# Attention scores: the second pass over the keys on 64 contraction rows, two heads side by side

## The chip, the cores and the metric

The kernel runs on one core of a Trainium2 chip. The metric is the device time of one execution in microseconds (us). Engines are named as in the profile: PE is TensorE's matmul stream and PEld its weight load, DVE is VectorE, ACT is ScalarE, POOL is GpSimd, and SP issues the DMAs.

## What is computed

The reference is two layers of a hybrid block over 2048 latent tokens and 256 context tokens of width 1024. Each layer normalises and modulates its input, projects it, runs three groups of heads in parallel (windowed attention, Fourier mixing, a short convolution), gates and concatenates them, and projects the result back with a residual add. The change is in the attention, whose core is this:

```python
def window_attention(q, k, v, kc, vc, sink_b):
    ...
    qb = (q * (HEAD_DIM ** -0.5)).reshape(b, nb, BLOCK, KV_HEADS, Q_PER_KV, HEAD_DIM).transpose(1, 0, 2, 3, 4, 5)
    ...
    def one_block(args):
        ...
        s_loc = jnp.einsum('bqkgd,bnkd->bkgqn', qi, ks).astype(jnp.float32)
        s_loc = jnp.where(valid, s_loc, -jnp.inf)
        s_ctx = jnp.einsum('bqkgd,bnkd->bkgqn', qi, kc).astype(jnp.float32)
        p = sink_softmax(jnp.concatenate([s_ctx, s_loc], axis=-1), sink_b).astype(v.dtype)
        return (jnp.einsum('bkgqn,bnkd->bqkgd', p[..., :nc], vc)
                + jnp.einsum('bkgqn,bnkd->bqkgd', p[..., nc:], vs))
```

There are 8 query heads of 64 dimensions, which share 2 key/value heads (four query heads each). A block is 128 query tokens. It sees all 256 context keys and its own block with the neighbour on each side: 384 local keys, or 256 at the two ends of the sequence. In the first layer the 256 context tokens are updated too, as two blocks that see the context keys alone.

## The kernel before, in words

**Precision.** Matmul operands are of type fp32r, whose products are less exact than fp32. Each operand is therefore split into hi and lo (`split`, L79: hi is the rounded copy, lo the rest), and a product is formed as hi*hi + hi*lo + lo*hi, three matmuls (`proj_k`, L274). For the attention scores the split is folded into the contraction: a head has only 64 dimensions, and the array contracts 128 rows. So q is stored in DRAM with hi in rows 0 to 63 and lo in rows 64 to 127 of every head (`store_hl`, L299; `dst` is `qs`, 128 rows x 8 heads x tokens). The keys are loaded twice, once into rows 0 to 63 and once into rows 64 to 127 (`open_ep` L1033 for the context keys, `kseg` L1211 for the local ones), each copy with hi and lo as separate planes, index `x`.

**Scores.** `u_qk` (L1067) makes the scores of one block and one key/value head, four query heads `hh` in turn. For each it takes a PSUM tile `sp` of two banks and runs two passes over the context keys (L1078, 256 columns) and two over the local keys (L1081, 384 or 256 columns). With x = 0 all 128 rows contract [q hi; q lo] with key hi in both halves, with x = 1 the same rows contract with key lo. Then DVE reads the tile once, adds the mask and finds the row maximum (L1088), and ACT takes the exponential (L1091). After the fourth head POOL scales by the reciprocal of the sums (L1102).

**Order.** Layer by layer there are two phases: `half` (projections, Fourier mixing, convolution) and `phase2` (attention and output projection). In `phase2` every stage runs several generators whose calls are interleaved by a string; one letter is one call:

```python
ORDER = "bAACCBCcBCABBACBBCBBCcACBCBB"
```

A is `u_qk` of the current unit (block and key/value head), B is `u_pv` of the unit before (transposes of the probabilities L1127, their split on ACT and DVE, the product with the values L1140 and L1141), C is `u_out` (output projection L1176 to L1178, norm, residual); small letters are the same generators of the stage before, being finished. So PE gets its instructions in an order written out by hand, and it runs them in that order. The A calls stand at places 2, 3, 11, 14 and 23: the first four are the four heads, the last takes the reciprocal and has POOL scale. The first stages and the last have strings of their own of the same kind.

**PSUM.** There are two `sp` tiles; each is free again when DVE has read it (L1088). `tp` has two banks, `op` and `yp` one each, and that fills PSUM.

Of the kernel before, what the change touches and what calls it, by code (L numbers as in the profile page):

```python
# [8 lines left out]
F32 = mybir.dt.float32  # L9
# [54 lines left out]
def f(t):  # L64
    return t.bitcast(F32)


class Kern:
# [230 lines left out]
    def store_hl(self, hi, lo, dst, tok, n, kq):  # L299
        nc = self.nc  # L300
        if kq is None:
            for v in range(2):
                for x, t in enumerate((hi, lo)):
                    nc.sync.dma_start(dst[:, v, x, tok:tok + n], f(t[v * 64:(v + 1) * 64, :n]))
        else:
            for v in range(2):
                for x, t in enumerate((hi, lo)):
                    nc.sync.dma_start(dst[x * 64:(x + 1) * 64, kq + 4 * v, tok:tok + n], f(t[v * 64:(v + 1) * 64, :n]))

    def qk_chunk(self, l, st, a, n, tok, kq, rope):  # L310
        nc = self.nc
# [755 lines left out]
    def u_qk(self, p, ps, B, kv):  # L1067
        nc = self.nc
        nm = p.tile([128, 4], F32, name="nm", tag="nm", bufs=2)
        sm = p.tile([128, 4], F32, name="sm", tag="sm", bufs=2)  # L1070
        B.pts = getattr(B, "pts", {})
        B.pts[kv] = []
        W, nl = B.W, B.nl
        for hh in range(4):
            h = kv * 4 + hh
            sp = ps.tile([128, 1024], F32, name="sp", tag="sp")
            for x in range(2):
                nc.tensor.matmul(sp[:, 256:512], B.q[:, h, :], self.kctx[:, kv, x, :], start=(x == 0), stop=(x == 1))  # L1078
            if nl:
                for x in range(2):  # L1080
                    nc.tensor.matmul(sp[:, 512:512 + nl], B.q[:, h, :], B.seg[:, kv, x, B.k0:B.k0 + nl],  # L1081
                                     start=(x == 0), stop=(x == 1))
            pt = p.tile([128, 640], F32, name="pt", tag="pt", bufs=8)[:, :W]
            d, x, m = pt, sp[:, 256:256 + W], self.mask[:, :W]
            if nl and B.qb == 0:
                d, x = [t.rearrange("p (a b) -> p a b", a=2) for t in (d, x)]
                m = self.mask.rearrange("p (a b) -> p a b", a=2)[:, :, :256]
            nc.vector.tensor_tensor_reduce(d, x, m, scale=-0.125,  # L1088
                                           scalar=self.nsink[:, h:h + 1], op0=ALU.add, op1=ALU.min,
                                           accum_out=nm[:, hh:hh + 1])  # L1090
            nc.scalar.activation(pt, pt, AF.Exp, bias=nm[:, hh:hh + 1], scale=-1.0, accum_out=sm[:, hh:hh + 1])  # L1091
            B.pts[kv].append(pt)
            if hh == 3:
                es = p.tile([128, 4], F32, name="es", tag="es", bufs=2)
                nc.gpsimd.tensor_tensor(es, nm, self.nsink[:, kv * 4:kv * 4 + 4], op=ALU.subtract)
                nc.scalar.activation(es, es, AF.Exp, bias=0.0, scale=1.0)
                nc.gpsimd.tensor_tensor(es, es, sm, op=ALU.add)
                yield
                rv = p.tile([128, 4], F32, name="rv", tag="rv", bufs=2)
                nc.vector.reciprocal(rv, es)  # L1100
                for g in range(4):
                    nc.gpsimd.tensor_scalar(B.pts[kv][g], B.pts[kv][g], rv[:, g:g + 1], 1.0, op0=ALU.mult, op1=ALU.mult)  # L1102
            yield
# [389 lines left out]
```

## Time and profile before

| | |
|---|---|
| time, median of 3 runs | 2089.26 us (2084.22 to 2091.58) |
| profiled execution, span | 2093.9 us |
| PE busy | 1980.6 us, 95% |
| DVE busy | 1233.3 us, 59% |
| second phase, first layer (676 to 1200 us) | PE 509.63 of 524 us |
| second phase, second layer (1646 to 2094 us) | PE 429.75 of 448 us |
| score matmuls, context keys (L1078) | 544 |
| score matmuls, local keys (L1081) | 512 |

The span is the time from the first to the last instruction of one execution under the profiler; the page gives no other time of that execution. Busy time of PE is taken from recorded matmuls whose ends are modelled and overlap the next matmul, so what a matmul takes in a dense stretch is read from the distance between two starts.

### The profile page before, as it was taken

The page shows a single profiled execution, that of the slowest core. Times are in us where ns is not written, and L with a number is a line of the kernel's source. Part 1 is how long each engine was busy: PE and PEld are TensorE (multiplying, and loading weights), DVE is VectorE, ACT ScalarE, POOL GpSimd, SP SyncE. Part 2 cuts the span into 40 slices and gives each one's busy share as a digit, 9 for nine tenths or more (in the row PEclk, how much of TensorE's full clock was granted, in tenths as well). Part 3 has the DMA queues.
Part 4 walks back from the last instruction along what each step waited for, and adds up shares of the span by engine and source line. Part 5 has one row for each costly group of instructions (what it writes and reads, how often), then busy time and mean ns, then how long its engine had stood idle before and what let it go on. Part 6 is the DMA issues. An engine that isn't in the chain of part 4 may idle for free.

```text
span 2093.9 us, 28506 instructions
## 1 busy us (share of the span) xinstructions
PE 1980.6 (95%) x10218; PEld 1671.9 (80%) x10218; DVE 1233.3 (59%) x2218; ACT 855.5 (41%) x1745; POOL 748.0 (36%) x967
## 2 busy tenths in 40 slices
PE   6787999999999899999999999999999989999998
PEld 2686877788788688888887888888887778888886
DVE  7343876445552677777777614333554277777775
ACT  6241211321322556666666412132222266666663
POOL 4221322231432444444444414233243254444443
PEclk9899999999999999999999999999999999999999
DMA  7678666444735744433332625124564654434421
GB/s 303 114 192 223 188 211 219 140 154 137 210 127 163 207 116 122 120 106 106 103 104 106 206 80 130 61 95 122 157 186 136 178 157 113 106 107 111 117 75 41
DMA packets 190333, 295.68 MB, mean 141 GB/s; under 512 B 17624, under 2 KB 121840, under 8 KB 189168
## 3 DMA queue, kind: packets, MB, share of 16 engines
q1 hardware_dynamic: 190192, 293.87, 47.8%
q8 instruction: 80, 1.31, 0.3%
q14 instruction: 61, 0.50, 0.1%
HBM read 218.43 MB, written 75.39 MB: 140 GB/s over the span
## 4 chain that ended last, share of the span: by engine, by line
PE 69%; DMA 10%; DVE 10%; issue 4%; POOL 3%; ACT 2%; SPq 1%; POOLq 0%; DVEq 0%; ACTq 0%
PE acc L280 8%; PE acc L279 8%; PE acc L278 8%; PE tp L1127 6%; PE yp L1176 6%; PE yp L1178 6%; PE yp L1177 6%; PE sp L1081 4%; PE op L1141 3%; PE op L1140 3%; PE sp L1078 3%; PE accb L378 2%; PE accb L376 2%; PE accb L377 2%; DVE jm L161 2%
## 5 line engine op out<-in xcount | busy, mean ns | idle before, releaser
L278 PE MATMUL acc<-big,wh 128*128 128x512 f32 x1152 | 458.9, 399 | 30.6 <-ACT big L267 11.5
L280 PE MATMUL acc<-big,wl 128*128 128x512 f32 x1152 | 454.6, 395 | 4.2 <-POOL wl L90 2.9
L279 PE MATMUL acc<-big,wh 128*128 128x512 f32 x1152 | 455.0, 395 | 0.4 <-POOL big L90 0.4
L90 POOL TENSOR_TENSOR wl<-wr,wh 128x1024 fp32r<-128x1024 f32 x63 | 158.4, 2515 | 400.5 <-ACT wh L84 272.7
L88 DVE TENSOR_TENSOR pl<-tp,ph 128x512 fp32r<-128x512 f32 x320 | 219.2, 687 | 105.6 <-ACT ph L84 102.5
L278 PEld LDWEIGHTS acc<-big,wh 128*128 128x128 f32 x1152 | 219.7, 191 | 75.2 <-ACT big L267 12.0
L1091 ACT ACTIVATE pt<-pt,nm 128x640 f32<-128x640 f32 (+2 forms) x272 | 216.2, 795 | 118.6 <-DVE nm L1088 118.2
L280 PEld LDWEIGHTS acc<-big,wl 128*128 128x128 f32 x1152 | 219.3, 190 | 51.8 <-POOL wl L90 4.0
L279 PEld LDWEIGHTS acc<-big,wh 128*128 128x128 f32 x1152 | 219.7, 191 | 43.7 <-POOL big L90 1.0
L84 ACT ACTIVATE ph<-tp 128x512 fp32r<-128x512 f32 x320 | 188.4, 591 | 132.6 <-PE tp L1127 126.2
L1102 POOL TENSOR_SCALAR pt<-pt,rv 128x640 f32<-128x640 f32 (+2 forms) x272 | 214.2, 808 | 27.2 <-DVE rv L1100 24.2
L1088 DVE CUSTOM_DVE_ANT_0 pt<-sp,mask,nsink 128x640 f32<-128x640 f32 (+2 forms) x256 | 213.4, 841 | 10.1 <-PE sp L1078 5.2
L1127 PE MATMUL tp<-ident,pt 128*128 128x128 f32 x1280 | 196.8, 274 | 12.7 <-POOL pt L1102 12.2
L1127 PEld LDWEIGHTS tp<-ident,pt 128*128 128x128 f32 x1280 | 158.6, 140 | 59.9 <-POOL pt L1102 19.2
L323 POOL TENSOR_TENSOR rs<-rs,sinT 128x512 f32<-128x512 f32 x40 | 68.1, 1703 | 183.6 <-DVE rs L321 154.1
L1081 PE MATMUL sp<-kseg,qt 128*128 128x384 f32 (+1 forms) x512 | 127.5, 330 | 1.1 <-DMA kseg<-ks 1.1
L1176 PE MATMUL yp<-big,hfh 128*128 128x512 f32 x272 | 118.1, 434 | 1.5 <-ACT big L84 1.5
L1078 PE MATMUL sp<-kctx,qt 128*128 128x256 f32 x544 | 114.2, 291 | 3.9 <-DMA qt<-qs 2.1
L1176 PE MATMUL yp<-big,hah 128*128 128x512 f32 x272 | 117.0, 431 | 0.0
L1078 PEld LDWEIGHTS sp<-kctx,qt 128*128 128x128 f32 x544 | 95.3, 189 | 18.4 <-DVE nm L1088 3.3
L1178 PE MATMUL yp<-big,hfl 128*128 128x512 f32 x272 | 107.5, 395 | 0.2
L1177 PE MATMUL yp<-big,hfh 128*128 128x512 f32 x272 | 107.1, 394 | 0.0
(373 smaller groups left out, 3711.5 us busy)
## 6 DMA issues: line engine op xcount, KB each, us to landing
wr<-in_wina SPq DMA_DIRECT2D x76, 512.0 KB, 3.8
qt<-qs SPq DMA_DIRECT2D x34, 512.0 KB, 5.0
wmt<-in_wmodt SPq DMA_DIRECT2D x32, 512.0 KB, 4.2
ftb<-ftd SPq DMA_DIRECT2D x36, 384.0 KB, 3.8
xt<-in_x SPq DMA_DIRECT2D x26, 512.0 KB, 6.4
kseg<-ks SPq DMA_DIRECT2D x24, 512.0 KB, 8.7
xt<-x SPq DMA_DIRECT2D x24, 512.0 KB, 4.5
gat<-gas SPq DMA_DIRECT2D x34, 256.0 KB, 3.2
```

The source lines that it names most:

```text
L88: self.last_v = nc.vector.tensor_tensor(lo, src, f(hi), op=ALU.subtract)
L278: nc.tensor.matmul(a, wh[:, k, :], hi[:, k, :n], start=(k == 0), stop=False)
L279: nc.tensor.matmul(a, wh[:, k, :], lo[:, k, :n], start=False, stop=False)
L280: nc.tensor.matmul(a, wl[:, k, :], hi[:, k, :n], start=False, stop=(k == KT - 1))
L1078: nc.tensor.matmul(sp[:, 256:512], B.q[:, h, :], self.kctx[:, kv, x, :], start=(x == 0), stop=(x == 1))
L1088: nc.vector.tensor_tensor_reduce(d, x, m, scale=-0.125, scalar=self.nsink[:, h:h + 1], op0=ALU.add, op1=ALU.min, accum_out=nm[:, hh:hh + 1])
L1091: nc.scalar.activation(pt, pt, AF.Exp, bias=nm[:, hh:hh + 1], scale=-1.0, accum_out=sm[:, hh:hh + 1])
L1102: nc.gpsimd.tensor_scalar(B.pts[kv][g], B.pts[kv][g], rv[:, g:g + 1], 1.0, op0=ALU.mult, op1=ALU.mult)
L1127: nc.tensor.transpose(tp[:, hh * 128:(hh + 1) * 128], pts[hh][:, t * 128:(t + 1) * 128], self.ident)
L1176: nc.tensor.matmul(yp, hh, wh[:, k, :], start=(i == 0), stop=False)
L1177: nc.tensor.matmul(yp, hh, wl[:, k, :], start=False, stop=False)
L1178: nc.tensor.matmul(yp, hl, wh[:, k, :], start=False, stop=(i == KT - 1))
```

## The change

The heads are taken in pairs, an even and an odd one. At the even head both `sp` tiles are taken, and PE gets the work of both heads: first the first pass of each over all 128 rows, then the second pass. The second pass contracts only q hi with key lo, on 64 rows; the product of q lo with key lo is no longer formed. So that the two heads lie in different halves of the array, `store_hl` writes hi of an odd head into rows 64 to 127 and lo into rows 0 to 63. For the first pass this makes no difference, since both halves of the keys hold the same. In the second pass the even head reads rows 0 to 63 and the odd head rows 64 to 127, and the matmuls of the two alternate: context keys of the even head, of the odd head, then local keys of each. At the odd head no matmul is left; the DVE and ACT work stays in its place.

```diff
@@ store_hl
-                    nc.sync.dma_start(dst[x * 64:(x + 1) * 64, kq + 4 * v, tok:tok + n], f(t[v * 64:(v + 1) * 64, :n]))
+                    r = (x + kq) % 2 * 64
+                    nc.sync.dma_start(dst[r:r + 64, kq + 4 * v, tok:tok + n], f(t[v * 64:(v + 1) * 64, :n]))
@@ u_qk
+        sps = {}
         for hh in range(4):
             h = kv * 4 + hh
-            sp = ps.tile([128, 1024], F32, name="sp", tag="sp")
-            for x in range(2):
-                nc.tensor.matmul(sp[:, 256:512], B.q[:, h, :], self.kctx[:, kv, x, :], start=(x == 0), stop=(x == 1))
-            if nl:
-                for x in range(2):
-                    nc.tensor.matmul(sp[:, 512:512 + nl], B.q[:, h, :], B.seg[:, kv, x, B.k0:B.k0 + nl],
-                                     start=(x == 0), stop=(x == 1))
+            if hh % 2 == 0:
+                for g in (hh, hh + 1):
+                    sp = sps[g] = ps.tile([128, 1024], F32, name="sp", tag="sp")
+                    q = B.q[:, kv * 4 + g, :]
+                    nc.tensor.matmul(sp[:, 256:512], q, self.kctx[:, kv, 0, :], start=True, stop=False)
+                    if nl:
+                        nc.tensor.matmul(sp[:, 512:512 + nl], q, B.seg[:, kv, 0, B.k0:B.k0 + nl], start=True, stop=False)
+                for g in (hh, hh + 1):
+                    r = slice(g % 2 * 64, g % 2 * 64 + 64)
+                    nc.tensor.matmul(sps[g][:, 256:512], B.q[r, kv * 4 + g, :], self.kctx[r, kv, 1, :],
+                                     start=False, stop=True)
+                if nl:
+                    for g in (hh, hh + 1):
+                        r = slice(g % 2 * 64, g % 2 * 64 + 64)
+                        nc.tensor.matmul(sps[g][:, 512:512 + nl], B.q[r, kv * 4 + g, :], B.seg[r, kv, 1, B.k0:B.k0 + nl],
+                                         start=False, stop=True)
+            sp = sps[hh]
```

## The prediction

> **What bounds the kernel now.** I read the summary first: which engine is full.
>
> ```profile
> span 2093.9 us, 28506 instructions
> PE 1980.6 (95%) x10218; PEld 1671.9 (80%) x10218; DVE 1233.3 (59%) x2218; ACT 855.5 (41%) x1745; POOL 748.0 (36%) x967
> ```
>
> PE, the matmul stream, is busy 95% of the span; PEld, its weight load, runs beside it. A matmul's recorded end is modelled, so only its start is used below. Next come the stretches in which the scores are computed, the second phase of each layer, from the view of busy time by stretches (core time, PE, PEld, DVE, ACT, POOL, clock, DMA share, GB/s).
>
> ```profile
> 676.00:1200.00 524.00, 509.63 (x2794) 430.73 (x2793) 386.55 (x719) 311.19 (x682) 234.24 (x424) 1.00 0.44 131
> ...
> 1646.00:2094.00 448.00, 429.75 (x2360) 363.74 (x2358) 314.78 (x590) 253.16 (x557) 184.41 (x336) 0.99 0.40 112
> ```
>
> PE has 14 us idle of 524 and 18 of 448, at full clock; the next engine, DVE, is at 70 to 74%. The chain of waits over 30 us inside names PE lines alone:
>
> ```profile
> by line: PE tp L1127 16.0%; PE yp L1176 15.6%; PE yp L1178 15.4%; PE yp L1177 15.3%; PE sp L1081 11.6%; PE op L1140 9.3%; PE op L1141 9.2%; PE sp L1078 7.9%
> ```
>
> So in these stages a nanosecond of PE's stream, gained or lost, is a nanosecond of time. The scores (L1078, L1081) are about a fifth of that stream, and half of them is the second pass.
>
> **The change part by part.** How many matmuls are touched stands in the groups, shapes kept apart:
>
> ```profile
> L1081 PE MATMUL sp<-kseg,qt 128*128 128x384 f32 x448 | 114.5, 336 | 0.0
> L1078 PE MATMUL sp<-kctx,qt 128*128 128x256 f32 x544 | 114.2, 291 | 3.9 <-DMA qt<-qs 2.1 <-DVE nm L1088 1.4 <-issue 0.4
> ...
> L1081 PE MATMUL sp<-kseg,qt 128*128 128x256 f32 x64 | 13.0, 285 | 1.1 <-DMA kseg<-ks 1.1
> ```
>
> One pair of heads has 4 context matmuls, so 544 make 136 pairs. 448/4 = 112 of these pairs have local keys of 384 columns, 64/4 = 16 of 256, and 8 (context blocks) have none. What a matmul really takes is the distance between starts in the timeline, not its recorded 291 or 336 ns:
>
> ```profile
> 901.67 0.40 PE L1078 MATMUL sp<-kctx,qt 128*128 128x256 f32 x2
> ...
> 901.91 0.51 PE L1081 MATMUL sp<-kseg,qt 128*128 128x384 f32 x2
> ...
> 902.26 0.40 PE L1078 MATMUL sp<-kctx,qt 128*128 128x256 f32 x2
> ...
> 902.50 0.51 PE L1081 MATMUL sp<-kseg,qt 128*128 128x384 f32 x2
> ...
> 902.85 0.40 PE L1176 MATMUL yp<-big,hfh 128*128 128x512 f32 x1
> ```
>
> Two of 256 columns take 0.24 us, 0.12 each; two of 384 take 0.35, 0.175 each. The second pass of a pair therefore costs 2 x 0.12 + 2 x 0.175 = 0.59 us now (0.48 with 256 local columns, 0.24 without local keys). The change keeps the number of matmuls and weight loads, but issues these four on 64 rows, heads alternating between the two halves of the array. If both halves stream at once, 0.59 becomes 0.295 (0.24, 0.12), a gain of as much.
>
> What it adds: PE goes from 128 rows to 64 and back once per pair. No 64-row matmul is in this trace. The nearest are the sixteen four-row ones of L667, in groups of four, and one group stands between full matmuls:
>
> ```profile
> 52.16 0.19 PEld L280 LDWEIGHTS acc<-big,wpl 128*128 128x128 f32 x1
> ...
> 52.40 0.40 PE L280 MATMUL acc<-big,wpl 128*128 128x512 f32 x1
> ...
> 52.73 0.32 PEld L667 LDWEIGHTS pmc<-ident,sg 4*128 4x128 f32 x4 [0.37 <-ACT jk L245]
> 52.73 0.41 PE L667 MATMUL pmc<-ident,sg 4*128 4x4 f32 x4
> 53.06 0.14 PEld L230 LDWEIGHTS pt<-ident,xt 128*128 128x128 f32 x1
> ```
> ```profile
> L667 PEld LDWEIGHTS pmc<-ident,sg x16: 133/136/138, 13.9 to 52.9; 4*128 4x128 f32 x16
> ```
> ```profile
> L662 ACT COPY sg<-pmr x2: 576/576/577, 43.1 to 50.8; 4x512 f32<-4x512 f32 x2
> ```
>
> A 512-column matmul streams 0.23 us (next fence: 237.02 to 237.25), so the L280 at 52.40 was through at 52.63. Its successor's load should start with it, at 52.40, as the load at 52.16 did with the matmul before it. It starts at 52.73: 0.10 after the stream's end. Its data can't be the reason, for the copy into sg began at 50.8 and takes 0.576. (The row blames an ACT operation that was over by 52.40; that leaves the rest unexplained.) On the way out, four loads span 0.32 with 0.136 for the last, so they start 0.06 apart and the last at 52.91; the full-row load follows at 53.06, 0.15 later in place of 0.06: another 0.09. Few columns alone don't do this; a transpose of 16 columns over all 128 rows was prefetched as any other:
>
> ```profile
> 237.02 0.39 PE L280 MATMUL acc<-big,wl 128*128 128x512 f32 x1
> 237.02 0.09 PEld L188 LDWEIGHTS pgt<-ident,gg 128*16 128x16 f32 x1
> 237.25 0.27 PE L188 MATMUL pgt<-ident,gg 128*16 128x128 f32 x1
> ```
>
> A load that isn't prefetched is paid in full. After short transposes such a one is seen:
>
> ```profile
> 904.56 0.19 PEld L1176 LDWEIGHTS yp<-big,hfh 128*128 128x128 f32 x1
> 904.59 0.48 PE L1176 MATMUL yp<-big,hfh 128*128 128x512 f32 x1
> ...
> 904.90 0.39 PE L1177 MATMUL yp<-big,hfh 128*128 128x512 f32 x1
> ```
>
> From the load to the next matmul's start are 0.34 us, of which 0.23 is the stream: the load took 0.11. So a switch costs 0.10 + 0.11 = 0.21 us, in and out 0.42 per pair. The bounds are 0 (64 rows behave as 128 do) and 0.42 (as four rows do); I take 0.42, since L667 is the one row here with part of the rows.
>
> "TensorEngine Tiling (Array Packing)" in the Trainium skill, Key Properties, speaks against this change too: changing the tiling mode, not just the tile, drains TensorE. It gives no price; by that rule the sum is the +19 us below and without it the -38 of the second rival, and the 0.10 us around L667 agrees with the rule.
>
> What the four matmuls take between the switches is bounded as well: 0.295 if both heads' loads and streams run side by side, 0.59 if nothing does. Between them is the case in which the streams overlap but four loads of 0.11 follow one another: loads end at 0.11, 0.22, 0.33, 0.44; the last local matmul starts at 0.44 and ends at 0.615, the first load included. I take 0.295 as the forecast's value, because the two halves share no rows; no row shows loads or streams of two row groups together.
>
> **The sum**: with 384 columns 0.42 - 0.295 = +0.125 us x 112 = 14.0; with 256 columns 0.42 - 0.24 = +0.18 x 16 = 2.9; context blocks 0.42 - 0.12 = +0.30 x 8 = 2.4. Together +19.3 us. Nothing hides it, as PE is the chain.
>
> What is moved: the fourth head's matmuls go ahead of two calls of the other generators, to the third's, and need the second head's PSUM buffer earlier.
>
> ```profile
> 904.62 0.88 DVE L1088 CUSTOM_DVE_ANT_0 pt<-sp,mask,nsink 128x640 f32<-128x640 f32 x1
> ...
> 906.50 0.40 PE L1078 MATMUL sp<-kctx,qt 128*128 128x256 f32 x2
> ```
>
> DVE has read that buffer by 905.50, and the pair starts at 906.50: 1 us of cover, nothing paid. If DVE slid past it, PE would stand with all the output projection's matmuls queued behind, and their ACT and DVE readers after them. Also, a first head's scores are ready only when the second's are, about 0.6 us later. DVE took the pair's first scores at 903.21, the new pair would be through near 901.67 + 1.30 = 902.97 plus the pipe: at most some tenths, hidden by the 1 us again. The stores of q swap row halves, with the same count and bytes; cost nothing.
>
> ```profile
> qs<-qh SPq DMA_DIRECT2D x64, 128.0 KB, 2.4
> ```
>
> **The rivals.**
> (a) Switch paid, little overlap. With loads in a row, a pair costs 0.10 + 0.615 + 0.10 + 0.11 - 0.59 = +0.335 x 112 = 37.5; with 256 columns the inner part is 0.56, +0.39 x 16 = 6.2; without local keys 0.34, +0.41 x 8 = 3.3: +47 us. With no overlap at all, the change not doing what it says, 0.42 x 136 = +57. For it: the 0.11 per load against 0.12 per context matmul leaves hardly room to overlap. Against: separate rows.
> (b) The other side, faster: no switch cost. Place: the same start of the pair's second pass; it decides at a switch below 0.147 us, half of 0.295. With full overlap -0.295 x 112 - 0.24 x 16 - 0.12 x 8 = -38 us, 2051. With loads in a row and one ahead, as full-row loads go now, the four take about 0.505, 0.45 and 0.23: -0.085 x 112 - 0.03 x 16 = -10 us, 2079. Against it: L667, entry and exit alike. For it: four rows may be another mode than 64. "TensorE: Matmul & The Clock Gate" (the Trainium skill), Part 3, has matmuls in distinct row groups start about 4 ns apart and names no switch cost; no run here shows it.
> (c) Neither: no switch cost and no overlap: 0 us, 2089.
>
> **How the numbers follow.** The profiled span, 2093.9, lies 4.6 over the median of 2089.26 (runs 2084.22 to 2091.58); the page shows no time around it. The sum is in absolute us of PE and I add it to the median: 2089.26 + 19.3 = 2108.6. Chances: forecast 0.32; (a) with loads in a row 0.21, without overlap 0.17; (b) full 0.13, in a row 0.09; (c) 0.08. The switch has thus 0.70, resting on one kind of row. Slower is 0.70, faster 0.22, same 0.08, where 0.3% (6 us) is about what a measurement here can tell from no change. The range leaves out full (b): from 2079 less the runs' spread of 7 us, 2072, to 2146 plus the same, 2153. The forecast alone would be 2100 to 2118.
>
> **What would show it.** In the timeline: the first 64-row load about 0.10 us after the full stream ends, not with its start; the two heads' matmuls starting within 0.06 us (overlap) or 0.11 and more (loads in a row); the next full-row load 0.10 us after the last 64-row stream. From first score matmul to the next full stream a pair takes 1.18 us now, 1.30 by the forecast, 1.51 and 1.60 by (a), 0.89 by (b). DVE waiting for the scores or PE for the buffer at over 10 us in the list of waits would say that the moved work counts. The forecast is wrong if the 64-row load starts with the full matmul ahead of it.

## The result, and the profile after

| | time, median | runs |
|---|---|---|
| kernel before | 2090.42 us | 4 (2084.22 to 2091.98) |
| kernel after | 2162.61 us | 4 (2158.92 to 2171.39) |

The ratio is 1.0361, 95% interval 1.0335 to 1.0387: 72 us slower, where 19 us were forecast and 2153 was the end of the range. The profiled execution of the kernel after took 2158.92 us, with a span of 2157.1.

Three things are read from the profile after: how busy PE is, what it waits for, and then one pair of heads at a time. First the summary of the kernel after:

```profile
span 2157.1 us, 28511 instructions
...
PE 2016.8 (93%) x10218; PEld 1638.8 (76%) x10218; DVE 1238.6 (57%) x2218; ACT 857.6 (40%) x1745; POOL 744.9 (35%) x967
```

PE's share fell from 95 to 93% though its busy time rose by 36 us (2016.8 - 1980.6). So there seem to be two losses: PE works longer, and PE stands more. The first is only a hint, because busy time rests on modelled ends: e3 below, which has no 64-row matmul, shows 2009.2 us, also 29 over before. The list of PE's waits (line waited for: us in total, times, longest) has a new first row in the kernel after:

```profile
PE sp L1082 <- DVE nm L1100: 44.9, 58, 2.5
```

The same wait in the kernel before, where the reading is L1088:

```profile
PE sp L1078 <- DVE nm L1088: 1.4, 1, 1.4
```

The first pass of a pair waits 58 times for DVE to have read the PSUM buffer. The chain of waits of the kernel after shows that this reaches the end, for POOL and DVE have grown in it from 3% and 10% in the kernel before:

```profile
PE 53%; DVE 15%; POOL 10%; DMA 9%; issue 9%; ACT 4%; SPq 2%; POOLq 0%; DVEq 0%; ACTq 0%
```

**A pair that does not wait** is the first of a unit. Timeline of PE, kernel after (start, duration, instruction, count; the start is what is read):

```profile
910.00 0.28 PE L1082 MATMUL sp<-kctx,qt 128*128 128x256 f32 x1
910.12 0.34 PE L1084 MATMUL sp<-kseg,qt 128*128 128x384 f32 x1
910.30 0.28 PE L1082 MATMUL sp<-kctx,qt 128*128 128x256 f32 x1
910.41 0.34 PE L1084 MATMUL sp<-kseg,qt 128*128 128x384 f32 x1
910.69 0.39 PE L1087 MATMUL sp<-kctx,qt 64*128 64x256 f32 x2
910.91 0.34 PE L1092 MATMUL sp<-kseg,qt 64*128 64x384 f32 x2
911.18 0.50 PE L1188 MATMUL yp<-big,hfh 128*128 128x512 f32 x1
911.52 0.39 PE L1189 MATMUL yp<-big,hfh 128*128 128x512 f32 x1
```

and of its weight loads:

```profile
910.30 0.19 PEld L1084 LDWEIGHTS sp<-kseg,qt 128*128 128x128 f32 x1
910.68 0.19 PEld L1087 LDWEIGHTS sp<-kctx,qt 64*128 64x128 f32 x2 [0.20 <-issue]
910.79 0.19 PEld L1092 LDWEIGHTS sp<-kseg,qt 64*128 64x128 f32 x2
```

The last full stream begins at 910.41 and takes 0.175, so it is through at 910.59; the 64-row loads start at 910.68, 0.10 later, and were not prefetched as the full-row load ahead of them was (idle 0.20, put down to "issue"). Two heads' loads together take as long as one (the two rows "x2" last 0.19 like the single loads), and the two matmuls of each "x2" start 3 to 4 ns apart. From the first 64-row matmul to the second kind are 0.22 us: 0.12 of stream and 0.10 of load. From there to the next full matmul are 0.27: 0.175 of stream, 0.09 of drain. That matmul then holds the array 0.34 instead of 0.23: another 0.11 of load. So in and out cost 0.10 + 0.10 + 0.09 + 0.11 = 0.40 us, and the two halves of the array work wholly side by side. With the exposed load the pair takes 1.18 + 0.11 = 1.29 us.

**A pair that waits** is the second of the same unit. PE, kernel after:

```profile
914.70 0.40 PE L1190 MATMUL yp<-big,hfl 128*128 128x512 f32 x1
915.78 0.39 PE L1082 MATMUL sp<-kctx,qt 128*128 128x256 f32 x1 [0.69 <-DVE nm L1100]
...
917.19 0.39 PE L1082 MATMUL sp<-kctx,qt 128*128 128x256 f32 x1 [0.85 <-DVE nm L1100]
...
918.17 0.51 PE L1152 MATMUL op<-ph,vctx 128*128 128x512 f32 x1
```

It starts 0.85 us after the stream ahead of it is through (914.70 + 0.23), and takes 2.39 us instead of 1.18: 2.06 us lost, or 1.95 without the 0.11 that the switch costs a pair that does not wait. The two rows name only 0.69 and 0.85 us of it, since they count from the modelled end of the matmul ahead; so the 44.9 us of the list are less than what PE really stands. Why DVE is late stands in DVE's own timeline, kernel after:

```profile
910.00 0.69 DVE L1197 TENSOR_TENSOR z<-yp,GG 128x512 f32<-128x512 f32 x1 [0.79 <-ACT jk L1195]
912.79 1.28 DVE L1213 SCALAR_TENSOR_TENSOR xt<-z,rr,xt 128x1024 f32<-128x1024 f32 x1 [2.10 <-POOL rr L104]
914.11 0.69 DVE L1162 TENSOR_TENSOR at<-op,ht 64x512 f32<-64x512 f32 x1
914.84 0.88 DVE L1100 CUSTOM_DVE_ANT_0 pt<-sp,mask,nsink 128x640 f32<-128x640 f32 x1
...
916.25 0.88 DVE L1100 CUSTOM_DVE_ANT_0 pt<-sp,mask,nsink 128x640 f32<-128x640 f32 x1
```

against the same stretch of the kernel before:

```profile
901.67 0.69 DVE L1185 TENSOR_TENSOR z<-yp,GG 128x512 f32<-128x512 f32 x1 [0.73 <-ACT jk L1183]
902.48 0.69 DVE L1150 TENSOR_TENSOR at<-op,ht 64x512 f32<-64x512 f32 x1
903.21 0.89 DVE L1088 CUSTOM_DVE_ANT_0 pt<-sp,mask,nsink 128x640 f32<-128x640 f32 x1
...
906.98 1.27 DVE L1201 SCALAR_TENSOR_TENSOR xt<-z,rr,xt 128x1024 f32<-128x1024 f32 x1
```

DVE's order is another. The residual add (`xt`, L1201 before and L1213 after, the same text) stood behind both readings of the scores; now it stands ahead of them, right behind `z`. It needs `rr`, the norm's factor, which POOL makes, and POOL (kernel after) has the four scalings of the probabilities first:

```profile
907.43 3.14 POOL L1114 TENSOR_SCALAR pt<-pt,rv 128x640 f32<-128x640 f32 x4 [0.31 <-DVE rv L1112]
...
912.57 0.19 POOL L104 TENSOR_TENSOR rr<-ry,rt 128x1 f32<-128x1 f32 x1
```

So DVE stands 2.10 us, works 1.28 on the add, and reads the scores 4.84 us after the start of `z` (914.84 - 910.00) instead of 1.54 (903.21 - 901.67). Of these 3.3 us one was covered, and of the other 2.3 PE loses the 1.95. In DVE's list of waits, between 676 and 2060 us of the kernel after, this is

```profile
DVE xt L1213 <- POOL rr L104: 54.3, 26, 2.8
```

(61.7 us in 30 over the whole span), and in the kernel before, over the whole span:

```profile
DVE xt L1201 <- POOL rr L104: 4.6, 3, 2.6
```

It happens about once per block, in every second unit. Neither the string of calls nor the text of the add differs between the kernels; the order within DVE's queue is laid out by the planner, the part of the framework that places each engine's instructions when a program is built. Why it moved the add, the runs do not show.

**Theory**: the pairing itself costs about what was forecast (+14 to +20 us: switch paid, overlap full), and the remaining 53 us come from the add's place on DVE. **Rivals**: (R1) the 64-row matmuls cost more than the one pair shows, the wait for DVE being a result of a slower PE; (R2) the pairing, with both buffers taken at once and the first head's scores ready later, is what makes DVE late, whatever its order; (R3) the overlap is only apparent, the records' starts being modelled.

### The profile page after: what moved, and what is told of

Read it like the earlier page. It is cut to its first block, busy times and chain, and to the rows that moved or that the text cites. A ratio compares the mean times of both kernels' runs of the same rounds, so it can differ in the third digit from the quotient of the medians.

```text
span 2157.1 us, 28511 instructions
## 1 busy us (share of the span) xinstructions
PE 2016.8 (93%) x10218; PEld 1638.8 (76%) x10218; DVE 1238.6 (57%) x2218; ACT 857.6 (40%) x1745; POOL 744.9 (35%) x967
## 4 chain that ended last, share of the span: by engine, by line
PE 53%; DVE 15%; POOL 10%; DMA 9%; issue 9%; ACT 4%; SPq 2%; POOLq 0%; DVEq 0%; ACTq 0%
PE acc L278 8%; PE acc L280 8%; PE acc L279 8%; POOL pt L1114 5%; PE tp L1139 3%; PE yp L1188 3%; PE yp L1190 3%; PE yp L1189 3%; DVE pt L1100 2%; PE op L1152 2%; PE op L1153 2%; PE accb L379 2%; PE accb L377 2%; PE accb L378 2%; DVE jm L161 2%
## 5 line engine op out<-in xcount | busy, mean ns | idle before, releaser
L84 ACT ACTIVATE ph<-tp 128x512 fp32r<-128x512 f32 x320 | 188.4, 592 | 157.5 <-PE tp L1139 152.3
L1139 PEld LDWEIGHTS tp<-ident,pt 128*128 128x128 f32 x1280 | 157.6, 140 | 53.7 <-POOL pt L1114 12.2
L1082 PE MATMUL sp<-kctx,qt 128*128 128x256 f32 x272 | 82.1, 306 | 47.0 <-DVE nm L1100 44.9
L1188 PE MATMUL yp<-big,hfh 128*128 128x512 f32 x272 | 123.3, 453 | 0.9 <-DVE z L1197 0.9
L1107 POOL TENSOR_TENSOR es<-nm,nsink 128x4 f32<-128x4 f32 x68 | 14.4, 212 | 314.5 <-DVE nm L1100 314.5
L1188 PE MATMUL yp<-big,hah 128*128 128x512 f32 x272 | 122.0, 449 | 0.0
L1190 PE MATMUL yp<-big,hal 128*128 128x512 f32 x272 | 106.9, 394 | 0.0
L1082 PEld LDWEIGHTS sp<-kctx,qt 128*128 128x128 f32 x272 | 51.1, 188 | 73.5 <-DVE nm L1100 64.9
```

The source lines that it names most:

```text
L84: nc.scalar.activation(hi, src, AF.Copy, bias=0.0, scale=1.0)
L1139: nc.tensor.transpose(tp[:, hh * 128:(hh + 1) * 128], pts[hh][:, t * 128:(t + 1) * 128], self.ident)
L1188: nc.tensor.matmul(yp, hh, wh[:, k, :], start=(i == 0), stop=False)
L1190: nc.tensor.matmul(yp, hl, wh[:, k, :], start=False, stop=(i == KT - 1))
```

## The experiments

**e1, the readings first.** The kernel after with the add queued behind the newest reading of scores. By the traces the orders of PE and POOL stay as they are. On DVE 28 of the adds move and nothing else does. On ACT 28 copies of the transposes (`ph`, L84) move too, from ahead of the exponential of the first of the two heads to behind it, where the kernel before has them.

```diff
-            nc.vector.tensor_tensor_reduce(d, x, m, scale=-0.125,
+            self.last_rd = nc.vector.tensor_tensor_reduce(d, x, m, scale=-0.125,
...
-                nc.vector.scalar_tensor_tensor(B.xo, B.z, r, B.xo, op0=ALU.mult, op1=ALU.add)
+                with self.tc.issue_after(self.last_rd.ins):
+                    nc.vector.scalar_tensor_tensor(B.xo, B.z, r, B.xo, op0=ALU.mult, op1=ALU.add)
```

> The changed kernel, and DVE's residual add (xt from z and rr) is queued behind the newest reading of the scores, where it stood before the change; PE's order and every amount of work stay. Theory: in the changed kernel DVE holds that add ahead of the scores' reading, waits there for POOL (54 us in 26 waits in the trace), and PE waits for the score buffers. Then about 2162 - 54 = 2108 us, 0.8% over before, PE's wait for the buffers near 0, and what is left, 16 us, is 136 pairs at 0.40 us for the switches less 0.295 us from the overlap. Rival 1: PE waits because a pair needs both score buffers at once; then the time stays near 2160. Rival 2: the 64-row mode makes the scores late; near 2160 as well.

Measured 2109.64 us (2104.35 to 2112.56) against 2088.72 of the kernel before; ratio 1.0097, 1.0074 to 1.0119, or +20 us. PE's wait for the readings in the second phases (from 676 us) is

```profile
PE sp L1082 <- DVE nm L1100: 3.3, 2, 2.5
```

and DVE's wait for `rr` at the add fell to 4.2 us in 2. In this trace DVE reads the scores 1.54 us after the start of `z` again (906.88 - 905.34). So 53 us of the 72 (55 by the two ratios) go with the add's place: R2 falls, and so does R1 for all but the +20. The time alone could not tell the add from ACT's copies; the wait can, for DVE's 2.10 us ahead of the add end with POOL's `rr`. PE's order is the same in both kernels, so their matmuls can also be compared start by start (worked out from all recorded matmuls): the kernel after takes 22.4 us longer from a projection matmul to a score matmul behind it, and 33.6 us longer from one score matmul to the next, 56.0 together where the spans differ by 49.0.

**e2, e1 on full rows.** As e1, and the second pass contracts all 128 rows again, so that the pairs stay and the switch goes.

```diff
-                    nc.tensor.matmul(sps[g][:, 256:512], B.q[r, kv * 4 + g, :], self.kctx[r, kv, 1, :],
+                    nc.tensor.matmul(sps[g][:, 256:512], B.q[:, kv * 4 + g, :], self.kctx[:, kv, 1, :],
...
-                        nc.tensor.matmul(sps[g][:, 512:512 + nl], B.q[r, kv * 4 + g, :], B.seg[r, kv, 1, B.k0:B.k0 + nl],
+                        nc.tensor.matmul(sps[g][:, 512:512 + nl], B.q[:, kv * 4 + g, :], B.seg[:, kv, 1, B.k0:B.k0 + nl],
```

> As the run before, and the second pass on all 128 rows (with the product lo times lo again), in the same order of pairs: no 64-row matmul, no switch, no overlap. Theory: the switches less the overlap are worth 16 us, so about 2092 us, within 0.3% of before. Rival 1 (both buffers at once): near 2145 to 2160. If the 64-row mode were free in itself and something else of the pairing cost time, it would be as slow as the run before.

Measured 2091.42 us (2087.03 to 2099.14, 10 runs), ratio 1.0014, 0.9999 to 1.0029. Taking the heads in pairs is free; the 64 rows cost the 18 to 20 us between e2 and e1. The two have the same order on PE, DVE, ACT and POOL, so their score sections can be laid side by side: from the first score matmul of each section to the second full one behind it, over all sections, e1 takes 215.1 us and e2 194.6, a difference of 20.5 (worked out from the starts of all recorded matmuls). 11.3 of it are the 116 sections with a whole pair, 0.10 each; 9.2 are the rest, context blocks and pairs of the first and last stages that other matmuls cut in two, so that each part pays a switch.

**e3, full rows in the planner's own order.** The kernel after with the edit of e2 alone.

> The changed kernel with its own order of DVE, and the second pass on all 128 rows: the pairing alone. Theory: the pairing brings the residual add ahead of the scores' reading, whatever the rows: about 2092 + 54 = 2146 us, 2.7% over before, with PE waiting for DVE at the score buffers some 45 us. Rival 2 (the 64-row mode makes the scores late): about 2092.

Measured 2159.55 us (2156.43 to 2161.72), ratio 1.0334, 1.0311 to 1.0356: no 64-row matmul in it, and yet 70 us slower than before. Its order is that of the kernel after on PE, DVE, ACT and POOL, so it is the pairing, and not the 64 rows, with which the planner moves the add. Its list of PE's waits (second phases) shows it:

```profile
PE sp L1082 <- DVE nm L1100: 46.6, 58, 2.6
```

The expectation was 13 us too low. The two costs do not simply add: the order costs 68 us on full rows (e3 less e2) and 53 with the switch (after less e1), and the switch 18 us without this order (e1 less e2) and 3 us with it (after less e3, whose intervals overlap). Why is not shown. It could be that a PE that waits for DVE anyway pays the switch out of its wait, but the wait is only 1.7 us shorter in the kernel after than in e3, and its score sections take 17 us longer (247.4 against 230.3, worked out as for e2). Part of it may be the clock: the runs of e3 were granted 0.975 to 0.981, those of the kernel after 0.980 to 0.982. What this order of DVE would cost without the pairing was not run.

**e4, both heads on the same rows.** As e1, but q is stored as before the change, hi of every head in rows 0 to 63, and the second pass of both heads uses these rows. Matmuls, shapes and switches stay; only the two halves can't work side by side.

```diff
-                    r = (x + kq) % 2 * 64
+                    r = x * 64
...
-                    r = slice(g % 2 * 64, g % 2 * 64 + 64)
+                    r = slice(0, 64)
...
-                        r = slice(g % 2 * 64, g % 2 * 64 + 64)
+                        r = slice(0, 64)
```

> As the first of these runs, but both heads' second pass uses rows 0 to 63 (q is stored as before the change): the switches stay and the overlap goes. Theory: 112 x 0.295 + 16 x 0.24 + 8 x 0.12 = 38 us more than the first run, about 2146 us; the matmuls of the two heads start 0.12 and 0.175 us apart. If the overlap were worth less than it looks, nearer 2108.

Measured 2142.54 us (2138.08 to 2150.59), ratio 1.0261, 1.0233 to 1.0290, which is 33 us above e1 where 38 were expected. Timeline of PE, e4:

```profile
901.37 0.50 PE L1087 MATMUL sp<-kctx,qt 64*128 64x256 f32 x2
901.71 0.51 PE L1092 MATMUL sp<-kseg,qt 64*128 64x384 f32 x2
902.15 0.50 PE L1188 MATMUL yp<-big,hfh 128*128 128x512 f32 x1
```

From the first 64-row matmul to the next full one are 0.78 us, against 0.49 (910.69 to 911.18) in the kernel after. The difference, 0.29, is the second head's streams, 0.12 + 0.175. The overlap is real, as it shows in the time too, and R3 falls.

**e5, two switches per pair.** As e1, but the context keys of the pair are finished in both passes before its local keys begin, so that a pair goes to 64 rows and back twice.

```diff
+                for part in range(2 if nl else 1):
+                    for g in (hh, hh + 1):
+                        sp, q = sps[g], B.q[:, kv * 4 + g, :]
...
+                    for g in (hh, hh + 1):
...
+                        sp, q = sps[g], B.q[r, kv * 4 + g, :]
+                        if part == 0:
+                            nc.tensor.matmul(sp[:, 256:512], q, self.kctx[r, kv, 1, :], start=False, stop=True)
+                        else:
+                            nc.tensor.matmul(sp[:, 512:512 + nl], q, B.seg[r, kv, 1, B.k0:B.k0 + nl], start=False, stop=True)
```

> As e1_reads_first, and each pair goes to 64 rows and back twice: context keys first pass, second pass, then local keys first pass, second pass. Theory: a switch in and out costs 0.40 us of PE (0.10 drain and 0.10 exposed load each way), so 128 pairs x 0.40 = 51 us more than that run's 2109.6, about 2161 us. Rival: the cost is one of the pairing and not of the switches; then it stays at 2110.

Measured 2160.24 us (2152.17 to 2166.92), ratio 1.0340, 1.0308 to 1.0373: 51 us above e1. Over 128 pairs with local keys that is 0.40 us for one switch in and out, what the single pair gave. Timeline of PE, e5:

```profile
899.16 0.40 PE L1085 MATMUL sp<-kctx,qt 128*128 128x256 f32 x2
899.49 0.39 PE L1092 MATMUL sp<-kctx,qt 64*128 64x256 f32 x2
899.80 0.62 PE L1087 MATMUL sp<-kseg,qt 128*128 128x384 f32 x2
900.35 0.44 PE L1094 MATMUL sp<-kseg,qt 64*128 64x384 f32 x2
900.72 0.50 PE L1189 MATMUL yp<-big,hfh 128*128 128x512 f32 x1
```

From 899.49 to 899.80 are 0.31 us for 0.12 of stream: a drain and a load.

**e6 to e11, is there a version that gains?** If a switch costs 0.40 and four halved streams give back 0.295, a section on 64 rows pays once more work of that kind stands in it. The transposes of the unit before (`tp`, 128x128 each) can be done in halves of 64 rows, two halves side by side. In e6 the first pair of a unit keeps its 64-row pass, and 16 such halves, in place of eight full transposes, go into the same section; the second pair is on full rows again. It starts from e1, and the calls are moved so that the section comes late enough:

```diff
-ORDER = "bAACCBCcBCABBACBBCBBCcACBCBB"
+ORDER = "bBAACCCcBCABBACBBCBBCcACBCBB"
...
+                for hh in range(4):
+                    for x in range(2):
+                        r = slice(x * 64, x * 64 + 64)
+                        c = t * 256 + hh * 64
+                        nc.tensor.transpose(tps[x][:, c:c + 64], pts[hh][r, t * 128:(t + 1) * 128], self.ident[r, r])
```

> From e1_reads_first: the first pair of a unit keeps the 64-row second pass, and the transposes of the first two key tiles of the unit before are put beside it in 64-row halves (64 columns each, the two halves into two PSUM banks); their split is done in four pieces in place of two; the second pair goes back to full rows, head by head. Theory: a switch pays if enough stands between its two ends. Per stage 0.295 (scores) + 8 x 0.108 - 8 x 0.06 = 0.38 (transposes side by side) + 2 x 0.085 (loads that stood exposed after transposes) - 0.40 (switch) = -0.45 us of PE x 60 stages = -27 us: about 2063 us, 1.2% under before. Rival 1: transposes run no faster on half the rows, 2063 + 23 = 2086. Rival 2: DVE, with more and smaller pieces in another order, or POOL's scaling (transposes come 2 us earlier) ends last: 2090 or more, with PE waiting for them.

Measured 2115.99 us (2113.49 to 2118.29), ratio 1.0134, 1.0117 to 1.0151, far from the expected 2063. Timeline of PE, e6:

```profile
906.12 0.39 PE L1089 MATMUL sp<-kctx,qt 64*128 64x256 f32 x2
906.35 0.35 PE L1167 MATMUL tp<-ident,pt 64*128 64x64 f32 x6
907.06 0.28 PE L1167 MATMUL tp<-ident,pt 64*128 64x64 f32 x2 [0.37 <-POOL pt L1126]
907.15 0.42 PE L1095 MATMUL sp<-kseg,qt 64*128 64x384 f32 x2
907.41 0.41 PE L1167 MATMUL tp<-ident,pt 64*128 64x64 f32 x8
907.75 0.51 PE L1225 MATMUL yp<-big,hfh 128*128 128x512 f32 x1
```

The section now needs the probabilities that POOL is still scaling; over the second phases PE stands 27.6 us in 61 places there. And the expectation had counted the loads after the transposes twice: the 2 x 0.085 us are already in its 0.108 per transpose. That leaves 0.28 us per stage of its 0.45. Without its wait the section takes 1.89 us where pair and transposes took 2.06 before, 0.17 less. Of the missing 0.11, some 0.09 stand in the fence: the local keys' matmuls hold the array 0.26 us (907.15 to 907.41) where their stream is 0.175.

e7 and e8 move the section one and two calls later (`bBCAACCc...`, `bBCCAACc...`), to have it behind the scaling.

> e6_transposes_too with its first pair of scores one call of the output projection (three matmuls, 0.69 us) later, so that POOL's scaling is done when the 64-row transposes start. In that run PE waited 0.53 us per stage for POOL, 28 us in all, and the section from the first score matmul to the next projection took 1.89 us without the wait, against 2.06 for the same work in the kernel before. Theory: the wait goes, and what is left is a gain of 0.17 us x 60 stages = 10 us less the four switches of the early stages: about 2080 us, 0.4% under before. Rival: DVE or the score buffers, reached later, become the wait; 2090 or more.

> As the run before with the pair two calls (1.38 us) later. Theory: the same 2080 us if POOL was all that ended last; if the buffers of the second pair now wait for DVE (the pair's scores are read 0.7 us later than in the run before), some 0.3 us x 60 stages more, about 2098.

Measured 2110.34 us (ratio 1.0093, 1.0070 to 1.0115) and 2112.07 us (1.0096, 1.0071 to 1.0122). The wait for POOL at this line fell to 6.0 and 3.9 us, but the planner put three full matmuls of the output projection into the section. Timeline of PE, e7:

```profile
828.92 0.38 PE L1089 MATMUL sp<-kctx,qt 64*128 64x256 f32 x1
829.24 0.50 PE L1225 MATMUL yp<-big,hfh 128*128 128x512 f32 x1
...
830.13 0.39 PE L1089 MATMUL sp<-kctx,qt 64*128 64x256 f32 x1
```

That is a second switch, and the first head's second pass over the context keys runs alone. So the order of the calls does not fix PE's order either: here the planner moved matmuls into the section, which is one call. e9 holds the section together: e7 with PE's order around it pinned, and the first stages on full rows.

> e7_pair_one_call_later, with PE's order held: the output projection's three matmuls go ahead of the pair, and nothing comes between the pair's first score and its last 64-row transpose (in e7 the three matmuls stood inside the 64-row part, which made a second switch in and out); the early stages of each layer keep full rows. Theory: one switch per stage, no wait for POOL: per stage 2.06 us of PE before and 1.89 now, -0.17 x 60 = -10 us: about 2080 us, ratio 0.995. Rival: DVE, whose readings of the scores come 0.69 us later, makes the second pair wait for its buffers: 2090 or more.

Measured 2141.63 us (2135.32 to 2142.84), ratio 1.0234, 1.0218 to 1.0249. The list of PE's waits in the second phases, e9:

```profile
PE yp L1233 <- DVE z L1242: 26.8, 34, 3.6
PE yp L1233 <- POOL pt L1132: 16.8, 25, 0.7
```

With the order fixed, the projection stands in line for its only PSUM bank and for a section that waits for POOL. So the cause in e6 was to be taken away where it is: e10 is e6, with the first stages on full rows and the scaling of the fourth head on ACT instead of POOL.

```diff
-                for g in range(4):
+                nc.scalar.activation(B.pts[kv][3], B.pts[kv][3], AF.Identity, bias=0.0, scale=rv[:, 3:4])
+                for g in range(3):
```

> e6_transposes_too, with the fourth head's scaling on ACT in place of POOL, so that all four heads are scaled 0.8 us earlier, and full rows in the early stages of each layer; order of PE as in e6. Theory: POOL's end was the one wait there (0.53 us per stage), so it goes and the section's 0.17 us per stage remain: 2090 - 60 x 0.17 = 2080 us, ratio 0.995. Rival: ACT, which takes the 0.8 us ahead of the copy that frees the projection's bank, or DVE ends last then, 2090 or more.

Measured 2094.38 us (2088.49 to 2099.19, 12 runs), ratio 1.0019, 1.0008 to 1.0031. One large wait is left, in every second unit; e10, PE's waits:

```profile
PE tp L1168 <- POOL pt L1127: 12.2, 31, 2.5
```

e11 gives ACT the third head as well.

> As e10, but ACT scales the probabilities of the third and fourth head and POOL those of the first two. In e10 the one wait left in the section was that of the transposes for POOL's scaling, 12.2 us in 31 places. If that wait was all that kept e10 at the time of the kernel before, it goes and the time falls by 10 to 12 us: 2080 to 2084, ratio about 0.996. If the scaling is only moved to the end of a queue on ACT that is as late, the transposes wait there instead (for the ACT line of the scaling, or for the exponential of the next unit), and the time stays at 2092 to 2098. The computation is that of e10.

Measured 2089.56 us (2084.59 to 2096.39, 12 runs) against 2086.69; ratio 1.0013, 1.0000 to 1.0027. The wait fell to 2.2 us in 4, and another, smaller one came; e11, PE's waits:

```profile
PE yp L1227 <- DVE z L1236: 8.2, 26, 0.4
```

So 10 us of one wait went and 8 of another came, and the time is that of the kernel before, within what can be told. No version that was run beats the kernel before. That the waits are what swallows the section's 10 us is not shown: the kernel before waits for POOL's scaling too (12.2 us in 17 places), and PE's idle time ahead of the score, transpose, value and projection matmuls adds up to 22 us there and 23 us in e11. The kernel before with its scaling shared between POOL and ACT was not run. In e1 and e4 to e11, as in the kernel after, the lo*lo product is left out for the pairs that use 64 rows.

## Why the prediction was right or wrong

**The bound** (PE's stream is the time in these stages): right for e1, where 20.5 us more in the score sections became +20 us of time. It was not a fixed property of the kernel: in the kernel after PE stands 45 us for DVE.

**The switch**, forecast 0.10 + 0.11 each way, 0.42 in and out, from four-row matmuls: measured 0.40 in one pair and 0.40 as the slope of e5. The Trainium skill, "TensorEngine Tiling (Array Packing)", Key Properties, says that a change of the tiling mode drains TensorE; the traces agree, with 0.09 to 0.10 us each way. Behind it a weight load of 0.10 to 0.11 us stands exposed.

**The overlap**, forecast as full because the halves share no rows: right. e4 puts it at 33 us of time, where the step had 38 in all, and at 0.29 in the pair shown, where it had 0.295. The same section of the Trainium skill has tiles load and multiply in parallel, and its page "TensorE: Matmul & The Clock Gate", Part 3, has matmuls in distinct row groups start about 4 ns apart; the records show 3 to 4 ns.

**The sum**, +19.3 us: e1 measures +20.3 by its ratio, inside an interval of 15 to 25. That it fits so well is partly luck, since two errors balance: a whole pair costs 0.10 and not 0.125 or 0.18, while the context blocks and the pairs that other matmuls cut in two, which the sum took for whole, cost 9.2 us, where the sum had 2.4 for the context blocks.

**What is moved**: this is the step that failed, a term put at nothing that cost 53 us. It read DVE's order in the trace of before, found 1 us of cover ahead of the second pair, and wrote "1 us of cover, nothing paid". That held only if DVE's queue kept its order, which nothing secured. The section on the kernel before says that PE runs its instructions in the order written out by hand; that does not hold throughout even for PE, as the pairs cut in two and e7 show, and DVE's order it does not fix at all. The residual add went ahead of the readings, and with it POOL's scaling into the path: 53 us (after less e1). The prediction named the outcome ("if DVE slid past it, PE would stand with all the output projection's matmuls queued behind") without giving it a price or a chance. The trace of before had the rows for one, POOL's above all:

```profile
900.12 3.15 POOL L1102 TENSOR_SCALAR pt<-pt,rv 128x640 f32<-128x640 f32 x4 [0.31 <-DVE rv L1100]
...
905.40 0.19 POOL L104 TENSOR_TENSOR rr<-ry,rt 128x1 f32<-128x1 f32 x1
```

With `rr` at 905.59, 1.27 us of add and 0.73 for `at`, DVE would have read the scores near 907.6 and not at 903.21: an estimate of 4.4 us, 3.4 behind the cover, where the pair shown lost 1.95. The prediction also named the view that would tell, PE waiting for the buffer at over 10 us: 44.9.

**The rivals**: (a), a switch with little overlap, would have given 2136 to 2146, and the kernel after lies above even that for another reason; e4, which has no overlap, measures 2142.54 against the 2146 worked out for it. (b) and (c) needed a free switch, which e5's +51 us excludes.

## What to carry to other kernels

When an edit moves work on one engine in a program whose queues a planner lays out, compare the order of the other engines' queues before pricing anything: one add per block that changed places on DVE cost more here (53 us) than the matmuls of the edit itself (20). Two heads in two row halves do halve the time of their streams, but one trip to 64 rows and back costs about 0.40 us at these shapes, so by an estimate from these figures it takes more than some 0.8 us of full-row matmuls in one section to gain (half of 0.8 is 0.40), and what is put there to fill the section brings its own producers along. Costs measured one by one need not add up: the order and the switch cost 68 and 18 us singly and 72 together.

## What the runs showed of the hardware

The prediction had left open whether 64 rows behave as four do. They do: both show 0.09 to 0.10 us of drain each way. Transposes by halves of 64 rows gain as the scores do. In the kernel before, four full ones stand in front of the projection matmul of 904.59 that the prediction shows:

```profile
904.23 0.60 PE L1127 MATMUL tp<-ident,pt 128*128 128x128 f32 x4
```

They take 0.36 us, and the matmul behind them 0.08 more than its stream, so 0.11 us for one. Two halves side by side start some 0.06 us behind the two before them (e6, within its section). That the gain of e6 never reached the time was due to what the section waits for; why e11, where that wait is nearly gone, has no gain either stays open.
